# A decoder trunk on one core: the gated norm's sums of squares with ones as the stationary operand, four groups on four quarters of a bank, and one set of roots per layer

## The chip, the cores and the metric

The kernel runs on one core of a Trainium2 chip. The metric is the device time of one execution in microseconds (us); less is better. TensorE (PE; its weight loads are listed apart as PEld), VectorE (DVE), ScalarE (ACT), GpSimd (POOL) and the DMA queues each work through their own instructions in order, and wait for each other through semaphores.

## The reference, cut to what matters

Two layers of a hybrid trunk over 256 tokens of 1024 channels. Each layer normalises the stream, projects it with one wide matrix, runs three token mixers side by side (a Mamba-2 scan, sliding-window attention, forgetting attention), projects each mixer's output to 1024 channels, merges them with sigmoid gates and adds an output projection to the stream. The change lies at the end of the Mamba branch, in its gated norm over four groups of 256 channels:

```python
def grouped_rms_norm(y, w, groups):
    b, s, d = y.shape
    yf = y.astype(jnp.float32).reshape(b, s, groups, d // groups)
    yf = yf * lax.rsqrt(jnp.mean(yf * yf, axis=-1, keepdims=True) + NORM_EPS)
    return (yf.reshape(b, s, d) * w.astype(jnp.float32)).astype(y.dtype)
...
    y = y.reshape(b, s, SSM_INNER) * jax.nn.silu(z)
    return grouped_rms_norm(y, norm_w, SSM_GROUPS)
...
        branch = jnp.einsum('bsiw,iwd->bsid', ys, w_proj[layer])
```

So each token needs one root for each of the four groups, eight numbers a partition when the 256 tokens lie as two tiles of 128.

## The kernel before, in words

**Weights.** Weight matrices come from HBM in pieces of 1024 numbers a partition (`raw`). Each piece is split into a rounded part on ScalarE (`hi`, line 268) and the rest on VectorE (`lo`, line 269), and each dense product is made of three passes over such parts. Six buffers each hold raw, hi and lo; four pieces at most are split ahead, and a piece is released when its last matmul is written down.

**Order.** TensorE's order is the program's. The dense units are written one behind the other. Smaller work (attention, the scan, the norms) is a generator: `launch` puts it on a list with a due time on a clock that `mm` and `transpose` (lines 90 to 101) add up, and `pump`, called within and behind dense units, lets due generators write their next step. `drain(br)` runs all that is left of one kind. The other engines' orders are set by a scheduler from priorities.

**The gated norm.** The eight units `u_z` of the Mamba branch (two blocks of 128 channels to a group) each multiply the scan's output, channels on partitions and 256 tokens along the row, by the gate and square it on ScalarE (line 850). Behind every second unit VectorE adds two squares into one (line 853), and `group_norm` is launched with a delay of 6.5 us. For one group it does, on TensorE, two fp32 matmuls of two columns (the squares of 128 tokens stationary, two columns of ones moving), so that the sums come out with tokens on partitions; then a scale on VectorE (line 866), a power of -0.5 on GpSimd (869), and three small steps on VectorE (871, 872, 874) that refine the root into the tile `gr`. Four groups in two layers make eight such sets.

**The projection.** Two gate units (512 columns, 128 tokens each; line 942 adds the bias, 943 is the tanh) stand between the last `u_z` and `u_proj_groups`, which first drains what is left of the norms. For each of two token tiles it makes the four groups' products, six dense matmuls of 512 columns each, alternately in the pools `mm` (three PSUM banks) and `mx` (five). ScalarE evicts the first group with its root as the scale (line 985), VectorE adds the other three with theirs (987). Then `merge` adds the branch to the others (1001 and 1002).

In the profile's names `ones` is the tile of ones, `L` any work tile, `mm` and `mx` PSUM banks, `pp` attention probabilities. An fp32 matmul leaves two records in the trace, a dense one (rounded parts) or a transpose leaves one.

Of the kernel before, what the change touches and what calls it, by code (L numbers as in the profile page):

```python
# [13 lines left out]
AF = mybir.ActivationFunctionType  # L14
ALU = mybir.AluOpType

P = 128
# [7 lines left out]
D_SOFT, D_SOFT2, D_EVAC, D_SSD, D_SSD2 = 7.0, 3.0, 3.0, 8.0, 3.0  # L25
D_K, D_Q, D_QK, D_G0, D_FOX, D_BDMA, D_BIAS = 6.0, 5.5, 2.0, 8.0, 0.0, 4.0, 2.0
D_SEL, D_CONST, D_NWB = 2.5, 1.5, 10.0
D_GN1, D_CUM, D_H, D_M = 6.5, 12.0, (4.8, 7.0), 5.0
BUDGET = 1.35
T_PP, T_SSD, T_BIAS = 1, 1, 1  # L30
N_RAW, N_SPLIT = 6, 6
# [13 lines left out]
def hybrid_trunk(  # L45
# [29 lines left out]
    def pmx():  # L75
        return PS("mx", 5)
# [14 lines left out]
    def mm(o, a, b, **kw):  # L91
        n = b.free_size()
        if a.dtype == F32R:
            clock["t"] += max(0.094, n / 2350.0)
        else:
            clock["t"] += max(0.2, n / 587.0) * (0.5 if a.free_size() == 64 else 1.0)
        nc.tensor.matmul(o, a, b, **kw)  # L97

    def transpose(o, a, i):
# [731 lines left out]
    def u_z(y, br, u, c):  # L831
        def f(w):
            p = chan(y, w, c)
            if u == 0 and br != 0:
                y.sz[br] = T("L8", [P, NK, S])
            if u == 0 and br == 0:
                y.yh[br] = T("L8", [P, 2, NK, P], F32R)
                y.yl[br] = T("L8", [P, 2, NK, P], F32R)
            th = T("L1", [P, S])
            act(halves(th), p, AF.Tanh, scale=0.5)  # L840
            y.zdone.add((br, u))
            if br != 0:
                stt(halves(y.sz[br][:, u, :]), halves(th), 1.0, p, op0=ALU.add, op1=ALU.mult)
            else:
                drain(0)
                sz = T("L1", [P, S])
                stt(halves(sz), halves(th), 1.0, p, op0=ALU.add, op1=ALU.mult)
                tt(y.xs[:, u, :], y.xs[:, u, :], sz, op=ALU.mult)
                sq = T("L1", [P, S])
                act(sq, y.xs[:, u, :], AF.Square)  # L850
                y.sq.append(sq)
                if u % 2 == 1:
                    tt(y.sq[-2], y.sq[-2], y.sq[-1], op=ALU.add)
                    launch(3 if u < 4 else 4, group_norm(y, u // 2, y.sq[-2]), D_GN1)
                yh, yl, src = y.yh[0][:, :, u, :], y.yl[0][:, :, u, :], halves(y.xs[:, u, :])
                act(yh, src, AF.Copy, scale=y.vec[:, 80 + u:81 + u])
                stt(yl, src, y.vec[:, 80 + u:81 + u], yh.bitcast(F32), op0=ALU.mult, op1=ALU.subtract)
            pump()
        return f

    def group_norm(y, g, q0):
        p = pmx()
        for t in range(2):
            mm(p[:, 2 * t:2 * t + 2], q0[:, t * P:(t + 1) * P], ones[:, 0:2], start=True, stop=True)
        v = T("sm", [P, 8])
        ts(v[:, 0:4], p[:, 0:4], 1.0 / 256, 4 * EPS, op0=ALU.mult, op1=ALU.add)  # L866

        r0 = T("sm", [P, 8])
        nc.gpsimd.tensor_tensor(r0[:, 0:4], v[:, 0:4], mhalf[:, 0:4], op=ALU.pow)  # L869
        a = T("sm", [P, 8])  # L870
        tt(a[:, 0:4], r0[:, 0:4], v[:, 0:4], op=ALU.mult)
        tt(a[:, 0:4], a[:, 0:4], r0[:, 0:4], op=ALU.mult)
        r = T("gr", [P, 4], bufs=4)
        stt(r, a[:, 0:4], -3.0, r0[:, 0:4], op0=ALU.add, op1=ALU.mult)
        y.gr[g] = r
        yield 0.0


# [89 lines left out]
    def u_proj_groups(y, c, t):  # L968

        def f(w):  # L970
            drain(3)
            drain(4)
            q = T("L2", [P, 512])
            for g in range(4):
                p = pmm() if g % 2 == 0 else pmx()
                n = 0
                for k in (2 * g, 2 * g + 1):
                    for a, b in ((y.yh[0], w.hi), (y.yl[0], w.hi), (y.yh[0], w.lo)):
                        mm(p, still(a, t, k), in_turn(b(k)), start=(n == 0), stop=(n == 5))
                        n += 1  # L980
                if w.last:
                    release(w, g + 1)
                r = y.gr[g][:, 2 * t:2 * t + 1]
                if g == 0:
                    act(halves(q), ordered(p), AF.Copy, scale=r)
                else:
                    stt(halves(q), ordered(p), r, halves(q), op0=ALU.mult, op1=ALU.add)
                if g == 1:
                    pump()
            merge(y, 0, c, t, halves(q))  # L990
            pump()
        return f
# [122 lines left out]
    for y in layers:  # L1115
        l = y.l
        w = w_in[l]
        y.gate, y.qT, y.ckT, y.sz, y.yh, y.yl, y.sq, y.h, y.ss, y.var, y.zdone, y.cqdone, y.gr = {}, {}, {}, {}, {}, {}, [], {}, {}, {}, set(), {}, {}

        def cols(c0, n=256):  # L1120
            return sub([(0, w[:, c0:c0 + n])], n)

        def z1(c0, br, b):
            op(cols(c0 + 256 * b), u_z(y, br, 2 * b, 0), u_z(y, br, 2 * b + 1, P))

        def zs(c0, br):
            for b in range(4):
                z1(c0, br, b)

        def gates_proj(br):  # L1130
            def g(b):
                c = 512 * b
                op(cols(C_G + D * br + c, 512), u_gate(y, br, c, 0), u_gate(y, br, c, 1))

            def p(b):
                c = 512 * b
                if b == 0 and br != 0:
                    op(None, lambda y=y: split_late(y, br))
                i = sub([(0, w_proj[l, br, :, c:c + 512])], 512)
                if br == 0:  # L1140
                    op(i, u_proj_groups(y, c, 0), u_proj_groups(y, c, 1))
                else:
                    op(i, u_proj(y, br, c, 0), u_proj(y, br, c, 1))
            seq = [(g, 0), (p, 0), (g, 1), (p, 1)]
            if br == 0:
                seq = [(lambda b: z1(C_ZA, 0, b), b) for b in range(4)] + seq
            return [lambda f=f, b=b: f(b) for f, b in seq]

        if l == 0:
            k, v = cols(C_BK), cols(C_BV)  # L1150
            op(k, u_bkv(y, 0, 0, [lambda j=j: second_rows(j) for j in range(2)]))
            op(k, u_bkv(y, 0, 1))
            op(v, u_bkv(y, 256, 0), u_bkv(y, 256, 1))
            op(None, lambda: layer_consts(y0))
            for c in (0, 2):
                op(cols(C_BQ + 256 * c, 512), u_bq(y, c, 0), u_bq(y, c, 1))
        else:
            kv, q0 = cols(C_BK, 512), cols(C_BQ)
            op(None, lambda: drain(5))
            op(kv, u_bkv(y, 0, 0))  # L1160
            op(q0, u_bq(y, 0, 0))
            op(None, lambda: drain(6))
            op(kv, u_bkv(y, 0, 1))
            op(q0, u_bq(y, 0, 1))
            for c, n in ((1, 512), (3, 256)):
                op(cols(C_BQ + 256 * c, n), u_bq(y, c, 0), u_bq(y, c, 1))
        op(None, lambda y=y: layer_vec(y))
        op(sub([(0, w[:, C_DT:C_DT + 16]), (16, w[:, C_CF:C_CF + 16])], 32), u_small(y))
        zs(C_ZB, 1)
        heavy = [(C_B + 256 * b, 8 + 2 * b) for b in range(4)] + [(C_XS + 256 * b, 2 * b) for b in range(4)]  # L1170
        gp = gates_proj(1)
        lights = [lambda: None, lambda: op(cols(C_CV, 512), u_cv(y, 0, 0), u_cv(y, 0, 1))]
        lights += [lambda: None, lambda: op(cols(C_CV + 512, 512), u_cv(y, 512, 0), u_cv(y, 512, 1))]
        lights += [gp.pop(0), lambda: None, gp.pop(0), lambda: None]
        for (c0, u), light in zip(heavy, lights):
            op(cols(c0), u_conv(y, u, 0), u_conv(y, u + 1, P))
            light()
        for f in gp:
            f()

        for b, zb in enumerate(((), (0,), (1,), (2, 3))):
            op(cols(C_CK + 256 * b), u_ck(y, 2 * b, 0), u_ck(y, 2 * b + 1, P))
            op(cols(C_CQ + 256 * b), u_cq(y, 2 * b, 0), u_cq(y, 2 * b + 1, P))
            if b == 1:
                op(None, load_final if l + 1 == L else lambda: layer_consts(layers[1]))
            for z in zb:
                z1(C_ZC, 2, z)
        for f in gates_proj(0):
            f()
        for f in gates_proj(2):  # L1190
            f()
        o = [sub([(0, w_out[l, :, c:c + n])], n) for c, n in ((0, 256), (256, 512), (768, 256))]
        pieces_out[l] = o[0]
        op(o[0], u_out2(y, 0))
        for t in range(2):
            for i, c in ((1, 256), (2, 768)):
                op(o[i], u_out(y, c, t, i))
# [91 lines left out]
```

## Time and profile before

| | us |
|---|---|
| median of 3 runs (834.16 to 834.62) | 834.62 |
| the profiled execution | 834.18 |
| its span | 832.3 |
| TensorE busy | 820.6 |
| VectorE busy | 656.4 |
| ScalarE busy | 504.6 |
| GpSimd busy | 127.2 |

The span is the time from the first to the last instruction; 1.9 us of the profiled execution lie around it. A row of the profile's timeline has the start, the length from the first start to the last end of like instructions in a row, the engine, the line, and the operation with what it writes and reads, partitions by elements (for a matmul rows*columns of the array that are in use, then what is moved), the count, and, where the engine sat idle before, for how long and what ended it. Layer 1 repeats layer 0's stage about 407 us later.

### The profile page before, as it was taken

What the parts mean: (1) busy time and instruction counts of PE and PEld (TensorE: products, weight loads), DVE (VectorE), ACT (ScalarE), POOL (GpSimd) and SP (SyncE); (2) the same over time, 40 slices, a digit from 0 to 9 for tenths busy, and PEclk for the clock granted to TensorE, in tenths of its full rate; (3) what the DMA queues carried; (4) which work ended last, traced back from release to release, by engine and by line L of the source; (5) the groups of instructions that cost most, each with busy time, mean ns of one, the idle gap of its engine ahead of it and who ended that gap; (6) DMA issues with size and microseconds to landing.
All of it is one profiled execution on the core that took longest, in us unless ns stands there. A gap on an engine that the chain in (4) does not pass through costs nothing.

```text
span 832.3 us, 15656 instructions
## 1 busy us (share of the span) xinstructions
PE 820.6 (99%) x5800; PEld 748.7 (90%) x5800; DVE 656.4 (79%) x1355; ACT 504.6 (61%) x970; POOL 127.2 (15%) x167
## 2 busy tenths in 40 slices
PE   7999999999999999999999999999999999999996
PEld 7999888989999998888989998898899999988896
DVE  5788997998776788875788889889968668888665
ACT  6566777665666675543555667775457666655442
POOL 7411300000130211100014121000003110121000
PEclk9999999999999999999999999999999999999999
DMA  9946564567474756676687575456756565667632
GB/s 301 273 147 184 179 202 165 176 217 227 131 208 136 240 167 189 216 216 201 209 245 216 146 212 174 152 182 196 244 165 185 167 181 150 189 216 215 215 104 74
DMA packets 123739, 158.39 MB, mean 190 GB/s; under 512 B 12800, under 2 KB 84208, under 8 KB 123664
## 3 DMA queue, kind: packets, MB, share of 16 engines
q1 hardware_dynamic: 109456, 140.79, 55.3%
q10 hardware_dynamic: 14160, 16.49, 6.7%
q8 instruction: 45, 0.74, 0.4%
q14 instruction: 30, 0.25, 0.1%
q0 software_dynamic: 48, 0.13, 0.0%
HBM read 155.22 MB, written 2.16 MB: 189 GB/s over the span
## 4 chain that ended last, share of the span: by engine, by line
PE 97%; DMA 1%; ACT 0%; DVE 0%; POOL 0%; SPq 0%; issue 0%; POOLq 0%
PE mm L97 83%; PE mx L97 11%; PE mx L101 4%; DMA raw<-in_w_in_dram 1%; POOL lo L1221 0%; ACT hi L1220 0%; ACT L L1079 0%; DVE L L269 0%; ACT L L268 0%; POOLq L1285 0%; ACT L L219 0%; DVE L L1062 0%; SPq L163 0%; DVE L L1067 0%; SPq L164 0%
## 5 line engine op out<-in xcount | busy, mean ns | idle before, releaser
L269 DVE TENSOR_TENSOR lo<-raw,hi 128x1024 fp32r<-128x1024 f32 x252 | 310.1, 1243 | 71.0 <-ACT hi L268 65.3
L97 PE MATMUL mm<-hi,L 128*128 128x512 f32 (+1 forms) x1280 | 354.3, 363 | 1.9 <-ACT hi L1220 1.4
L268 ACT ACTIVATE hi<-raw 128x1024 fp32r<-128x1024 f32 x252 | 264.0, 1055 | 91.6 <-PE mm L97 77.5
L97 PE MATMUL mm<-L,hi 128*128 128x256 f32 x1792 | 316.9, 278 | 0.0
L97 PEld LDWEIGHTS mm<-L,hi 128*128 128x128 f32 x1792 | 277.5, 192 | 5.9 <-issue 3.4
L97 PEld LDWEIGHTS mm<-hi,L 128*128 128x128 f32 x1280 | 229.5, 190 | 30.9 <-issue 2.0
L97 PE MATMUL mm<-L,lo 128*128 128x256 f32 x896 | 246.4, 275 | 0.0
L97 PE MATMUL mm<-lo,L 128*128 128x512 f32 (+1 forms) x640 | 229.5, 360 | 0.2 <-POOL lo L1221 0.2
L97 PEld LDWEIGHTS mm<-L,lo 128*128 128x128 f32 x896 | 171.9, 192 | 0.2
L97 PEld LDWEIGHTS mm<-lo,L 128*128 128x128 f32 x640 | 121.3, 190 | 14.2 <-POOL lo L1221 0.5
L919 POOL TENSOR_SCALAR_AFFINE_SELECT bias<-bias 128x128 f32<-128x128 f32 x64 | 39.0, 642 | 268.9 <-DMA bias<-cumd 182.4
L779 DVE SCALAR_TENSOR_TENSOR L<-L,vec,L 128x255 f32<-128x255 f32 (+2 forms) x96 | 46.9, 489 | 6.4 <-ACT L L776 5.0
L97 PE MATMUL mx<-L,L 128*64 128x128 f32 (+1 forms) x384 | 36.5, 332 | 0.0
L97 PEld LDWEIGHTS mx<-L,L 128*64 128x64 f32 x384 | 23.8, 136 | 11.9 <-issue 2.7
L651 ACT ACTIVATE pp<-pp,nm 128x128 f32<-128x128 f32 x64 | 25.1, 393 | 13.6 <-DVE nm L644 13.5
L576 ACT ACTIVATE pp<-pp,nm 128x128 f32<-128x128 f32 x64 | 28.2, 443 | 8.3 <-DVE nm L570 8.3
L943 ACT ACTIVATE L<-L 128x512 f32<-128x512 f32 x24 | 15.0, 627 | 28.4 <-DVE L L942 28.1
L840 ACT ACTIVATE L<-mm 128x256 f32<-128x256 f32 x48 | 18.0, 376 | 20.6 <-PE mm L97 20.3
L782 ACT ACTIVATE L<-L 128x256 f32<-128x256 f32 x32 | 13.3, 417 | 26.6 <-DVE L L779 26.2
L676 POOL TENSOR_SCALAR_AFFINE_SELECT L<-L 128x256 f32<-128x256 f32 x16 | 10.3, 641 | 112.4 <-ACT L L674 112.4
L644 DVE CUSTOM_DVE_ANT_0 pp<-mx,wmask,nsink 128x128 f32<-128x128 f32 x64 | 24.1, 412 | 1.8 <-PE mx L97 1.8
L869 POOL TENSOR_TENSOR sm<-sm,mhalf 128x4 f32<-128x4 f32 x8 | 12.0, 1496 | 76.8 <-DVE sm L866 76.8
(181 smaller groups left out, 820.4 us busy)
## 6 DMA issues: line engine op xcount, KB each, us to landing
raw<-in_w_in_dram SPq DMA_DIRECT2D x200, 512.0 KB, 4.7
raw<-in_w_proj_dram SPq DMA_DIRECT2D x48, 512.0 KB, 4.5
raw<-in_w_out_dram SPq DMA_DIRECT2D x16, 512.0 KB, 5.0
L<-cumd ACTq DMA_DIRECT2D x8, 512.0 KB, 4.0
bias<-cumd ACTq DMA_DIRECT2D x16, 256.0 KB, 3.7
L<-in_gate_bias_dram ACTq DMA_DIRECT2D x12, 256.0 KB, 3.7
L<-in_x_dram SPq DMA_DIRECT2D x2, 512.0 KB, 4.8
nwb<-in_norm_w_dram SPq DMA_DIRECT2D x1, 512.0 KB, 5.3
```

What stands on the lines that cost most here:

```text
L97: nc.tensor.matmul(o, a, b, **kw)
L101: nc.tensor.transpose(o, a, i)
L268: keep(act)(hi, src, AF.Copy)
L269: keep(tt)(lo, src, hi.bitcast(F32), op=ALU.subtract)
L576: act(pp[:, i, sl], pp[:, i, sl], AF.Exp, scale=-1.0, bias=nm[:, e:e + 1], accum_out=sums[:, e:e + 1])
L644: nc.vector.tensor_tensor_reduce(out=pp[:, i, sl], in0=score(p, i, b), in1=m, scale=-0.125, scalar=ns[:, i:i + 1], op0=ALU.add, op1=ALU.mi ...
L651: act(pp[:, i, sl], pp[:, i, sl], AF.Exp, scale=-1.0, bias=nm[:, e:e + 1], accum_out=sums[:, e:e + 1])
L779: stt(a[:, s:S], x_[:, 0:S - s], y.vec[:, 16 * j + u:16 * j + u + 1], a[:, s:S], op0=ALU.mult, op1=ALU.add)
L782: act(th, a, AF.Tanh)
L840: act(halves(th), p, AF.Tanh, scale=0.5)
L919: nc.gpsimd.affine_select(out=bias[:, i, dst], in_=bias[:, i, src], compare_op=ALU.is_ge, fill=NEG, base=0, pattern=[[-1, P]], channel_mul ...
L943: act(g, g, AF.Tanh, scale=0.5)
```

## The change

`group_norms` takes the place of `group_norm`: it is launched once a layer, behind the last `u_z`. It keeps the four sums of squares until then. Four matmuls with 32 columns of ones as the stationary operand and 256 columns of a group's sums as the moving one write to the partitions 0 to 31, 32 to 63, 64 to 95 and 96 to 127 of one bank. ScalarE copies them, and at the next step two transposes bring the tokens to the partitions. One scale, one power and three small steps over 128x8 then make all eight roots, in place of four sets over 128x4. The clock that sets due times counts a matmul with 32 columns at a quarter, and the kind numbered 4 goes.

```diff
-D_GN1, D_CUM, D_H, D_M = 6.5, 12.0, (4.8, 7.0), 5.0
+D_GN1, D_GN2, D_CUM, D_H, D_M = 6.5, 2.5, 12.0, (4.8, 7.0), 5.0
...
-            clock["t"] += max(0.2, n / 587.0) * (0.5 if a.free_size() == 64 else 1.0)
+            clock["t"] += max(0.2, n / 587.0) * {64: 0.5, 32: 0.25}.get(a.free_size(), 1.0)
...
-                    launch(3 if u < 4 else 4, group_norm(y, u // 2, y.sq[-2]), D_GN1)
+                    if u == NK - 1:
+                        launch(3, group_norms(y), D_GN1)
...
-    def group_norm(y, g, q0):
+    def group_norms(y):
+        p = pmx()
+        for g in range(4):
+            mm(p[32 * g:32 * g + 32, 0:S], ones[:, 0:32], y.sq[2 * g], start=True, stop=True)
+        sums = T("L1", [P, S])
+        act(sums, p[:, 0:S], AF.Copy)
+        yield D_GN2
         p = pmx()
         for t in range(2):
-            mm(p[:, 2 * t:2 * t + 2], q0[:, t * P:(t + 1) * P], ones[:, 0:2], start=True, stop=True)
+            transpose(p[:, t * P:(t + 1) * P], sums[:, t * P:(t + 1) * P], ident)
         v = T("sm", [P, 8])
-        ts(v[:, 0:4], p[:, 0:4], 1.0 / 256, 4 * EPS, op0=ALU.mult, op1=ALU.add)
-
+        ts(v, p[:, 0:2 * P].rearrange("p (e r) -> p e r", r=32)[:, :, 0], 1.0 / 256, 4 * EPS,
+           op0=ALU.mult, op1=ALU.add)
         r0 = T("sm", [P, 8])
-        nc.gpsimd.tensor_tensor(r0[:, 0:4], v[:, 0:4], mhalf[:, 0:4], op=ALU.pow)
+        nc.gpsimd.tensor_tensor(r0, v, mhalf, op=ALU.pow)
         a = T("sm", [P, 8])
-        tt(a[:, 0:4], r0[:, 0:4], v[:, 0:4], op=ALU.mult)
-        tt(a[:, 0:4], a[:, 0:4], r0[:, 0:4], op=ALU.mult)
-        r = T("gr", [P, 4], bufs=4)
-        stt(r, a[:, 0:4], -3.0, r0[:, 0:4], op0=ALU.add, op1=ALU.mult)
-        y.gr[g] = r
+        tt(a, r0, v, op=ALU.mult)
+        tt(a, a, r0, op=ALU.mult)
+        y.gr = T("rs", [P, 8], bufs=4)
+        stt(y.gr, a, -3.0, r0, op0=ALU.add, op1=ALU.mult)
         yield 0.0
...
             drain(3)
-            drain(4)
...
-                r = y.gr[g][:, 2 * t:2 * t + 1]
+                r = y.gr[:, 4 * t + g:4 * t + g + 1]
```

**TensorE.** Before, in layer 0, the second of the four groups: an attention output (`mx_4101`, on 64 columns), the two matmuls of the norm, and the next dense unit.

```order
L97 MATMUL mm_4054<-L_25_153,hi_3889 128x256
L97 MATMUL mx_4101<-L_727_3945,L_273_1357 64x256 x2
L97 MATMUL mx_4101<-L_743_4033,L_273_1357 64x128 x2
L97 MATMUL mx_4101<-L_743_4033,L_273_1357 64x256
L97 MATMUL mx_4101<-L_745_4040,L_273_1357 64x256
L97 MATMUL mx_4101<-L_745_4040,L_273_1357 64x128 x2
L97 MATMUL mx_4111<-ones_86,L_725_3936 128x2 x2
L97 MATMUL mm_4123<-L_24_152,hi_3963 128x256
```

Now the norm's matmuls stand together in the middle of the second gate unit, three quarters through the two (`mm_4210`):

```order
L97 MATMUL mm_4210<-hi_4073,L_25_153 128x512
L97 MATMUL mm_4210<-lo_4074,L_24_152 128x512
L97 MATMUL mx_4235<-L_710_3844,ones_86 32x256
L97 MATMUL mx_4235<-L_725_3936,ones_86 32x256
L97 MATMUL mx_4235<-L_742_4027,ones_86 32x256
L97 MATMUL mx_4235<-L_759_4119,ones_86 32x256
L97 MATMUL mm_4210<-hi_4146,L_24_152 128x512
```

Twelve dense matmuls later come the transposes, ahead of the projection's first group (`mm_4282`):

```order
L97 MATMUL mm_4210<-hi_4164,L_24_152 128x512
L97 MATMUL mm_4210<-hi_4164,L_25_153 128x512
L97 MATMUL mm_4210<-lo_4165,L_24_152 128x512
L101 MATMUL mx_4269<-ident_71,L_782_4240 128x128 x2
L97 MATMUL mm_4282<-hi_4217,L_706_3837 128x512
L97 MATMUL mm_4282<-hi_4217,L_707_3838 128x512
```

The eight groups of two-column matmuls are gone; besides, the attention output `mx_4101` stands 24 dense matmuls later than it did. Nothing else of TensorE's order moves, and layer 1 is changed in the same way.

**ScalarE**, from the first gate's tanh (line 943 before, 949 now) to the projection's first eviction (985, now 990). Before:

```order
L268 ACTIVATE hi_4289<-raw_4071 128x1024
L943 ACTIVATE L_788_4243<-L_788_4243 128x512
L268 ACTIVATE hi_4301<-raw_4089 128x1024
L268 ACTIVATE hi_4353<-raw_4174 128x1024
L268 ACTIVATE hi_4367<-raw_4192 128x1024
L985 ACTIVATE L_808_4310<-mm_4311,gr_4052 128x512
```

Now, with the copy of the sums at line 867:

```order
L949 ACTIVATE L_773_4207<-L_773_4207 128x512
L268 ACTIVATE hi_4248<-raw_4059 128x1024
L268 ACTIVATE hi_4260<-raw_4077 128x1024
L867 ACTIVATE L_782_4240<-mx_4235 128x256
L1036 DMA L_922_4898<-in_x_dram 128x256
L1036 DMA L_925_4902<-in_x_dram 128x256
L268 ACTIVATE hi_4324<-raw_4150 128x1024
L268 ACTIVATE hi_4338<-raw_4168 128x1024
L1036 DMA L_951_5034<-in_x_dram 128x256
L1036 DMA L_972_5137<-in_x_dram 128x256
L949 ACTIVATE L_789_4266<-L_789_4266 128x512
L990 ACTIVATE L_795_4281<-mm_4282,rs_4279 128x512
```

The copy stands behind the second of four splits, the second gate's tanh has come ahead of the first eviction, and four loads of the stream (line 1031 before, then ahead of these rows) stand among them.

**VectorE**, from the splits of the projection's weights to its first scaled sum (line 987, now 992). Before, with the last group's scale and refinement (866, 871, 872, 874) among the splits:

```order
L269 TENSOR_TENSOR lo_4290<-raw_4071,hi_4289 128x1024
L866 TENSOR_SCALAR sm_4274<-mx_4271 128x4
L269 TENSOR_TENSOR lo_4302<-raw_4089,hi_4301 128x1024
L871 TENSOR_TENSOR sm_4278<-sm_4276,sm_4274 128x4
L269 TENSOR_TENSOR lo_4354<-raw_4174,hi_4353 128x1024
L872 TENSOR_TENSOR sm_4278<-sm_4278,sm_4276 128x4
L942 TENSOR_TENSOR L_807_4307<-mm_4246,L_786_4216 128x512
L874 SCALAR_TENSOR_TENSOR gr_4281<-sm_4278,sm_4276 128x4
L269 TENSOR_TENSOR lo_4368<-raw_4192,hi_4367 128x1024
L987 SCALAR_TENSOR_TENSOR L_808_4310<-mx_4319,gr_4121,L_808_4310 128x512
```

Now:

```order
L269 TENSOR_TENSOR lo_4249<-raw_4059,hi_4248 128x1024
L269 TENSOR_TENSOR lo_4261<-raw_4077,hi_4260 128x1024
L269 TENSOR_TENSOR lo_4325<-raw_4150,hi_4324 128x1024
L948 TENSOR_TENSOR L_789_4266<-mm_4210,L_771_4180 128x512
L873 TENSOR_SCALAR sm_4272<-mx_4269 128x8
L269 TENSOR_TENSOR lo_4339<-raw_4168,hi_4338 128x1024
L878 TENSOR_TENSOR sm_4276<-sm_4274,sm_4272 128x8
L879 TENSOR_TENSOR sm_4276<-sm_4276,sm_4274 128x8
L881 SCALAR_TENSOR_TENSOR rs_4279<-sm_4276,sm_4274 128x8
L992 SCALAR_TENSOR_TENSOR L_795_4281<-mx_4290,rs_4279,L_795_4281 128x512
```

The splits and the gate's sum keep their order; the scale comes behind the gate's sum with one split between it and the refinement, and the refinement's three steps stand together right ahead of the first scaled sum. The rows of the three earlier groups, further up, are gone.

More of the change, by code (lines that the diff above doesn't have):

```diff
@@ L1117, in hybrid_trunk @@
         w = w_in[l]
-        y.gate, y.qT, y.ckT, y.sz, y.yh, y.yl, y.sq, y.h, y.ss, y.var, y.zdone, y.cqdone, y.gr = {}, {}, {}, {}, {}, {}, [], {}, {}, {}, set(), {}, {}
+        y.gate, y.qT, y.ckT, y.sz, y.yh, y.yl, y.sq, y.h, y.ss, y.var, y.zdone, y.cqdone = {}, {}, {}, {}, {}, {}, [], {}, {}, {}, set(), {}
         def cols(c0, n=256):
```

## The prediction

> **What bounds the kernel now.** I read the busy shares first, then the chain that ended last, then TensorE's waits. The first two are on the page:
>
> ```profile
> span 832.3 us, 15656 instructions
> PE 820.6 (99%) x5800; PEld 748.7 (90%) x5800; DVE 656.4 (79%) x1355; ACT 504.6 (61%) x970; POOL 127.2 (15%) x167
> PEclk9999999999999999999999999999999999999999
> PE 97%; DMA 1%; ACT 0%; DVE 0%; POOL 0%; SPq 0%; issue 0%; POOLq 0%
> ```
>
> TensorE is busy for 99% of the span at the full clock, and 97% of the chain is TensorE's. The third view is TensorE's waits from 14 us to the end; these two lines are the whole answer:
>
> ```profile
> PE mm L97 <- ACT L L268: 0.2, 1, 0.2
> PE mm L97 <- DVE L L269: 0.2, 1, 0.2
> ```
>
> So after the start TensorE waits twice, 0.4 us in all (both at the turn of the layers). While that stays so, the span moves by what TensorE's own stream gains or loses. What the change does to VectorE, ScalarE and GpSimd counts only if it makes TensorE wait.
>
> **Term 1, what goes: eight groups of matmuls with two columns.** A busy time counts overlapping records twice, so I take prices from start times. This is the third group of layer 0, between two dense stretches:
>
> ```profile
> 311.07 0.28 PE L97 MATMUL mm<-L,hi 128*128 128x256 f32 x1
> 311.18 0.51 PE L97 MATMUL mx<-ones,L 128*128 128x2 f32 x4
> 311.55 0.68 PE L97 MATMUL mm<-hi,L 128*128 128x512 f32 x2
> 312.06 0.38 PE L97 MATMUL mm<-lo,L 128*128 128x512 f32 x1
> ```
>
> The group (two fp32 matmuls, two records each) starts at 311.18, and the third dense matmul behind it at 312.06, 0.88 us later. Two dense matmuls of 512 columns belong to that time. Their pitch is read from the stretch in the next fence: 102.29 to 102.94 is three of them, 0.217 each. So a group costs 0.88 - 0.43 = 0.45 us, though it streams two columns: with so few, the load of 128 weight columns is what takes the time. The first group, behind transposes, comes out the same:
>
> ```profile
> 300.60 0.51 PE L97 MATMUL mx<-ones,L 128*128 128x2 f32 x4
> 300.97 0.36 PE L97 MATMUL mm<-L,hi 128*128 128x256 f32 x1
> 301.16 0.28 PE L97 MATMUL mm<-L,lo 128*128 128x256 f32 x1
> ```
>
> From 300.60 to 301.16 is 0.56, less one dense matmul of 256 columns (0.11, as from 311.07 to 311.18): 0.45. Four groups a layer make **1.8 us**.
>
> **Term 2, what comes: four matmuls on quarters of the array.** The stationary operand is 32 columns of ones, the moving one 256 columns of sums. No row of before has four quarters at work. The nearest are the attention outputs, on halves (128*64), here between dense matmuls of 512:
>
> ```profile
> 100.00 0.38 PE L97 MATMUL mm<-lo,L 128*128 128x512 f32 x1
> 100.31 1.52 PE L97 MATMUL mx<-L,L 128*64 128x256 f32 x16
> 101.76 0.70 PE L97 MATMUL mm<-hi,L 128*128 128x512 f32 x2
> 102.29 0.38 PE L97 MATMUL mm<-lo,L 128*128 128x512 f32 x1
> 102.51 0.59 PE L97 MATMUL mm<-hi,L 128*128 128x512 f32 x2
> 102.94 0.38 PE L97 MATMUL mm<-lo,L 128*128 128x512 f32 x1
> ```
>
> From 100.00 to 102.29 is 2.29, less three dense matmuls (0.65): 1.64 us for eight fp32 matmuls of two records each, four of 256 columns and four of 128. What one record streams is read from transposes: six records of 128 columns from 299.95 to 300.60, 0.109 each.
>
> ```profile
> 299.95 0.82 PE L101 MATMUL mx<-ident,pp 128*128 128x128 f32 x6
> ```
>
> A record of 256 fp32 columns is then 0.218. One behind the other, the 16 records would take 8 x 0.218 + 8 x 0.109 = 2.6 us; two side by side take 1.31. The measured 1.64 is the second, plus 0.33 for going into the form with fewer columns and back. A close window shows how they stand beside each other:
>
> ```profile
> 303.82 0.44 PE L97 MATMUL mx<-L,L 128*64 128x256 f32 x2
> 303.82 0.65 PE L97 MATMUL mx<-L,L 128*64 128x256 f32 x4
> ```
>
> Two records that take 0.43 alone are both over 0.44 us after the first began, and four (both records of two matmuls) after 0.65. So the halves run side by side from the first record on.
>
> For four quarters there are then four prices, each with the 0.33: all four together, 2 x 0.218 + 0.33 = 0.77 us; two at a time, 4 x 0.218 + 0.33 = 1.20; a staircase in which each matmul's first record runs beside the second of the one before, 5 x 0.218 + 0.33 = 1.42; one after the other, 8 x 0.218 + 0.33 = 2.07. I take **0.77**, since nothing in the rows on halves sets a limit at two. The lower end, with the switch at nothing, is 0.44.
>
> Here a rule of the Trainium skill speaks against the change. The page "TensorE: Matmul & The Clock Gate", Part 3, says that matmuls start and end strictly in program order; for fp32 matmuls of two records that would make the staircase. The rows on halves disagree (two records within 0.01 us of each other at the start, where the second record of the same matmul can't be), unless the two records of a matmul are not neighbours in that order. The same part gives a measured speedup of 3.07 for four tiles; as an estimate by that figure the four would stream in 1.74 / 3.07 = 0.57 us instead of 0.44, and the saving would be 0.26 us smaller in all.
>
> **Term 3: two transposes a layer**, of the form above: 2 x 0.109 = **0.22 us**.
>
> **Sum.** A layer loses 1.8 and gains 0.77 + 0.22 = 0.99: 0.80 us less, **1.6 us for the two**. The rest of TensorE's order stays, but for one attention output that moves behind 24 dense matmuls; it stands between dense matmuls before and after. The profiled execution took 834.18 us, so 832.58. The runs lie at 834.16 and 834.62, the median at the upper; 1.6 off the median is 833.02. I predict **833.0**.
>
> **What hides the rest.** *The copy of the sums* on ScalarE (0.37 us, as the copies of 128x256 at L840) must end before the transposes, or TensorE waits. Between quarters and transposes stand twelve dense matmuls, 2.6 us. ScalarE's rows there before:
>
> ```profile
> 318.09 1.06 ACT L268 ACTIVATE hi<-raw 128x1024 fp32r<-128x1024 f32 x1 [1.74 <-PE mm L97]
> 319.06 0.61 ACT L943 ACTIVATE L<-L 128x512 f32<-128x512 f32 x1
> 319.58 1.04 ACT L268 ACTIVATE hi<-raw 128x1024 fp32r<-128x1024 f32 x1
> 321.17 1.07 ACT L268 ACTIVATE hi<-raw 128x1024 fp32r<-128x1024 f32 x1 [0.56 <-ACT hi L268]
> 322.47 1.06 ACT L268 ACTIVATE hi<-raw 128x1024 fp32r<-128x1024 f32 x1 [0.23 <-PE mm L97]
> 323.93 0.69 ACT L985 ACTIVATE L<-mm,gr 128x512 f32<-128x512 f32 x1 [0.41 <-PE mm L97]
> ```
>
> In the new order the copy stands behind the second split of this stretch. TensorE frees that split's buffer when the quarters begin; it takes 1.05, the copy 0.37, so the sums lie ready 1.5 to 1.8 us after the quarters began, against 0.77 + 2.6 = 3.4. **Cover: 1.6 us.** Without it, what is lacking would be TensorE's wait, once a layer.
>
> *The roots.* Before, three groups had theirs long ahead, and the last came as late as it could:
>
> ```profile
> 321.35 1.85 POOL L869 TENSOR_TENSOR sm<-sm,mhalf 128x4 f32<-128x4 f32 x1 [8.25 <-DVE sm L866]
> 323.24 0.16 DVE L871 TENSOR_TENSOR sm<-sm,sm 128x4 f32<-128x4 f32 x1 [0.90 <-POOL sm L869]
> 324.56 0.68 DVE L942 TENSOR_TENSOR L<-mm,L 128x512 f32<-128x512 f32 x1
> 325.23 1.22 DVE L269 TENSOR_TENSOR lo<-raw,hi 128x1024 fp32r<-128x1024 f32 x1
> 326.37 0.74 DVE L987 SCALAR_TENSOR_TENSOR L<-mx,gr,L 128x512 f32<-128x512 f32 x1
> ```
>
> Now all four need the transposes, and the first eviction (L985, ScalarE) waits for them. Counted from the transposes' start: up to 0.5 until they can be read, VectorE finishing a split and the gate's sum (1.22 + 0.68), the scale (0.15), the power on GpSimd (the rows of 128x4 run from 1.0 to 1.94; 128x8 is not in the trace, and I take 1.9), three small steps (0.5): about 4.9. ScalarE evicts by 5.6. TensorE needs that bank again only when the two others of the pool of three are filled, at the seventh group of six dense matmuls (every second group goes to the other pool): after 0.22 + 6 x 1.3 = 8.0 us. **Cover: 2.4 us.** Behind the waiting eviction ScalarE's queue holds the next split, and that one waited for TensorE anyway:
>
> ```profile
> 328.94 1.06 ACT L268 ACTIVATE hi<-raw 128x1024 fp32r<-128x1024 f32 x1 [3.04 <-PE mm L97]
> ```
>
> Three us idle there, so the split isn't late. VectorE's first scaled sum starts about 1 us later relative to TensorE; it had idle time of 0.5 us behind these sums, and its sixteen small steps and three waits on GpSimd become four steps and one wait.
>
> **The rivals.**
>
> *Fewer than four at once* (two at a time, or the staircase): 0.43 to 0.65 us dearer a layer, a saving of 0.3 to 0.7 us, **833.9 to 834.3**. For it: nothing in the trace has more than two. Against it: the halves show no trace of waiting for each other.
>
> *One after the other, the other side*: if quarters overlapped as little as matmuls on the full array do, a layer would pay 2.07 + 0.22 for the 1.8 it loses, 0.5 us more, and the time would be **835.6**, slower. It decides from 1.58 us for the four upward (1.8 - 0.22). Against it speak the halves.
>
> *Roots too late*: beyond the cover of 2.4 us each us costs one a layer. Two more splits of VectorE ahead of the small steps (2.4) and a power of twice the length (1.9) would bring 1.9 us of wait a layer, 3.8 - 1.6 = 2.2 us more than before, **836.8**. The new order has one split there, so this needs a stage that runs quite unlike before.
>
> *It doesn't do what it says*: the transposes wait for the sums. Beyond 1.6 us of cover; at 0.8 us of wait a layer the gain is gone, **834.6**.
>
> **How the numbers follow.** All four together 0.75; fewer at once 0.12; one after the other 0.05; roots too late 0.05; sums too late 0.03. The range runs from the lower end (0.44 for the four: 1.1 us a layer, 832.3, and 0.3 of the 0.46 us between the levels of the runs) to the staircase: **832.0 to 834.3**, which leaves out 0.13. A difference of 0.2%, 1.67 us, is about what a measurement of this kernel can tell from no change. My forecast of 1.6 lies just short of it, and the runs of before are 0.46 apart, so the likeliest case falls on both sides: **faster 0.40** (half of that case and little else), **same 0.53** (the other half, fewer at once, one after the other, sums late), **slower 0.07**.
>
> **What would show it.** The quarters' rows: eight records on 128*32 that start within 0.3 us if all four run together, and the third dense matmul behind them 0.77 + 0.43 us after the first of them. Transposes with no wait on ScalarE's copy. TensorE's waits still at 0.4 us. The eviction at L990 later relative to the projection's start by 2 to 4 us, with TensorE streaming through it. I am wrong if the quarters take over 1 us, or if TensorE waits for `mx<-ident,L` or on a bank in the first projection of the Mamba branch.

## The result and the profile after

The kernel after takes **832.86 us** (median of 16 runs, 832.35 to 834.32), the kernel before 834.26 in the same comparison (16 runs, 834.10 to 835.83). The ratio is **0.9981**, 95% interval 0.9974 to 0.9988: some 1.4 to 1.6 us, 1.6 having been forecast. The profiled execution took 832.96 us, 1.22 less than that of before; its span is 1.1 shorter (831.2 for 832.3).

The page of the kernel after, its span, the busy times and the chain that ended last:

```profile
span 831.2 us, 15603 instructions
PE 819.1 (99%) x5788; PEld 745.2 (90%) x5788; DVE 654.2 (79%) x1331; ACT 504.2 (61%) x972; POOL 121.1 (15%) x161
PE 96%; DMA 2%; DVE 1%; issue 0%; ACT 0%; POOL 0%; SPq 0%; POOLq 0%; DVEq 0%
```

TensorE is the bound as before. VectorE has 24 instructions and 2.2 us less to do, GpSimd six instructions and 6.1 us less; neither figure says anything of the time, since TensorE did not wait for either there.

TensorE's timeline around the new stage in layer 0 (start, length, engine, line, operation):

```profile
318.00 0.38 PE L97 MATMUL mm<-lo,L 128*128 128x512 f32 x1
318.31 0.64 PE L97 MATMUL mx<-L,ones 128*32 128x256 f32 x8
...
319.42 0.38 PE L97 MATMUL mm<-lo,L 128*128 128x512 f32 x1
...
321.36 0.38 PE L97 MATMUL mm<-lo,L 128*128 128x512 f32 x1
321.58 0.39 PE L101 MATMUL mx<-ident,L 128*128 128x128 f32 x2
...
322.24 0.38 PE L97 MATMUL mm<-lo,L 128*128 128x512 f32 x1
```

The price is read as in the prediction, by starts. From 318.00 to 319.42 is 1.42; three dense matmuls (0.65) belong to it, the first row's and two that are left out, so the four quarters cost **0.77**. From 321.36 to 322.24 is 0.88, less the same 0.65: the transposes cost **0.23**. The layer pays 1.00 for the 1.79 that it lost (four groups at 0.447). Layer 1 comes out the same within 0.01.

A window of 0.04 us, from 318.30 to 318.34, shows how many records have begun by then:

```profile
318.31 0.42 PE L97 MATMUL mx<-L,ones 128*32 128x256 f32 x4
```

Four, each some 7 ns behind the other in the trace's records; the other four (the second records of the same matmuls) begin together 0.24 us later. So four run at once, first all the first records and then all the second.

The saving is then 1.6 us for the two layers, and the span of the profiled execution shows 1.1. The rest went in two places. One is the start: the attention outputs that began at 100.31 before begin later, ahead of anything that was changed.

```profile
100.47 1.52 PE L97 MATMUL mx<-L,L 128*64 128x256 f32 x16
```

That is 0.16 us, and differs from execution to execution: in the second profile of the kernel after (e9_after) they begin at 100.30. TensorE's wait for GpSimd's split (line 1226, 0.8 us, until 16.00), the one new line in its waits from 14 us on, is part of the start too.

The other is **a new wait at the turn of the layers**, which the prediction did not have. With the later start, TensorE is 0.6 us ahead of before from the stage on, and a load of the residual stream is issued 0.6 us sooner, but it does not land 0.6 us sooner. ScalarE's queue in the kernel after issues it here (DMA issues are listed as ACTq):

```profile
410.56 0.45 ACTq L1036 DMA_DIRECT2D L<-in_x_dram  x1
```

VectorE's sum with it (line 1067) waits for the load, 5.7 us after the issue, and holds what stands behind it:

```profile
416.23 0.69 DVE L1067 TENSOR_TENSOR L<-mm,L 128x512 f32<-128x512 f32 x1 [0.53 <-DMA L<-in_x_dram]
...
417.97 0.68 DVE L269 TENSOR_TENSOR L<-mx,L 128x512 fp32r<-128x512 f32 x1
```

Behind it on VectorE stands its half of the next layer's token split (line 269), which ends at 418.65. TensorE needs that, and its weight load (listed apart as PEld) begins late, at 418.70 (the row names line 223, which ends only at 418.71); the matmuls show what it costs:

```profile
418.70 0.19 PEld L97 LDWEIGHTS mm<-hi,L 128*128 128x128 f32 x1 [0.36 <-DVE sm L223]
418.26 0.93 PE L97 MATMUL mm<-hi,L 128*128 128x512 f32 x2
419.03 0.38 PE L97 MATMUL mm<-lo,L 128*128 128x512 f32 x1
```

From 418.26 to 419.03 two matmuls take 0.77 us (0.76 unrounded), where 0.43 is their time: **0.33 us lost**. Of that, 0.23 lies ahead of the matmul that waited and 0.10 behind it: the next start follows it by 0.32 us and not by 0.217, as behind the waits of e5_late and e6_late_early below. Before, the load was issued at 411.19 and VectorE's sum began at 416.30 with no wait for it:

```profile
416.30 0.68 DVE L1062 TENSOR_TENSOR L<-mm,L 128x512 f32<-128x512 f32 x1
```

Together 1.60 - 0.16 - 0.33 = 1.11 us, against 1.12 by the spans. The other 0.10 of the 1.22 lies outside the span.

### The profile page after: what moved, and what is told of

The parts are those of the page before. It is cut to its first block, busy times and chain, and to the rows that moved or that the text cites. A ratio compares the mean times of both kernels' runs of the same rounds, so it can differ in the third digit from the quotient of the medians.

```text
span 831.2 us, 15603 instructions
## 1 busy us (share of the span) xinstructions
PE 819.1 (99%) x5788; PEld 745.2 (90%) x5788; DVE 654.2 (79%) x1331; ACT 504.2 (61%) x972; POOL 121.1 (15%) x161
## 4 chain that ended last, share of the span: by engine, by line
PE 96%; DMA 2%; DVE 1%; issue 0%; ACT 0%; POOL 0%; SPq 0%; POOLq 0%; DVEq 0%
PE mm L97 81%; PE mx L97 11%; PE mx L101 4%; DMA raw<-in_w_in_dram 1%; DMA L<-in_x_dram 1%; POOL lo L1226 0%; DVE L L269 0%; DVE lo L269 0%; ACT hi L1225 0%; DVE L L1067 0%; ACT L L219 0%; ACT L L1084 0%; ACT L L268 0%; POOLq L1290 0%; SPq L163 0%
## 5 line engine op out<-in xcount | busy, mean ns | idle before, releaser
L101 PE MATMUL mx<-ident,L 128*128 128x128 f32 x148 | 22.5, 275 | 0.3 <-DVE L L1237 0.3
```

Source lines behind the costliest of these rows:

```text
L101: nc.tensor.transpose(o, a, i)
```

## The experiments

**Theory A**: the gain is the difference of TensorE's own stream and nothing else; four quarters run at once and cost 2 x 0.218 + 0.33 us. **Theory B**, the rival: the gain comes from VectorE and GpSimd, which have one set of roots a layer to make in place of four. The edits are shown against the kernel after. Prices of stages are read by starts, as above: from the dense matmul ahead of the stage to the third start behind it, less three dense matmuls (0.65), of which two are left out of the rows. A wait is priced in the same way, up to the third start behind it. Layer 1 agrees within 0.01 us, unless it is said otherwise.

### e1_halves: the four sums on halves of the array

```diff
-            mm(p[32 * g:32 * g + 32, 0:S], ones[:, 0:32], y.sq[2 * g], start=True, stop=True)
-        sums = T("L1", [P, S])
-        act(sums, p[:, 0:S], AF.Copy)
+            mm(p[64 * (g % 2):64 * (g % 2) + 64, S * (g // 2):S * (g // 2) + S], ones[:, 0:64], y.sq[2 * g],
+               start=True, stop=True)
+        sums = T("L2", [P, 2 * S])
+        act(sums, p, AF.Copy)
...
-            transpose(p[:, t * P:(t + 1) * P], sums[:, t * P:(t + 1) * P], ident)
+            for j in range(2):
+                transpose(p[:, (2 * t + j) * P:(2 * t + j + 1) * P], sums[:, j * S + t * P:j * S + (t + 1) * P], ident)
...
```

> The four matmuls on halves of the array (64 columns of ones), two groups beside each other and two behind them, four transposes. Theory A (the gain is TensorE's stream alone, and the quarters run four at a time): the matmuls cost 4 x 0.218 + 0.33 = 1.20 us a layer in place of 0.77, the transposes 0.44 in place of 0.22, so 0.65 us more a layer and 1.3 us more than the change: 834.2, the gain over before (834.3) nearly gone. Theory B (the gain comes from the one set of roots: fewer small steps on VectorE and fewer waits on GpSimd): as the change, 832.9.

Measured: 833.92 us, ratio 0.9997 (0.9988 to 1.0006). TensorE's timeline of this kernel:

```profile
317.86 0.38 PE L97 MATMUL mm<-lo,L 128*128 128x512 f32 x1
318.16 1.08 PE L97 MATMUL mx<-L,ones 128*64 128x256 f32 x8
...
319.71 0.38 PE L97 MATMUL mm<-lo,L 128*128 128x512 f32 x1
```

From 317.86 to 319.71 is 1.85, less 0.65: 1.20, as "two at a time" gives, and 0.43 more than on quarters. The roots are batched here as in the kernel after, and nearly all of the gain is gone. That is theory A. The time lies 0.3 under the expected one, which was counted from the 832.9 of the kernel after, and so held that kernel's wait at the turn of the layers; this profile does not have it.

### e2_full: 128 columns of ones, one matmul after another

All four groups take the roots of the first here: the roots of the other three are left out.

```diff
-        p = pmx()
+        p, p2 = pmx(), pmx()
...
-            mm(p[32 * g:32 * g + 32, 0:S], ones[:, 0:32], y.sq[2 * g], start=True, stop=True)
+            mm((p, p2)[g // 2][:, g % 2 * S:g % 2 * S + S], ones, y.sq[2 * g], start=True, stop=True)
```

> The four matmuls on the full array (128 columns of ones), one behind the other, into two banks; the copy and the transposes as in the change, so that all four groups take the roots of the first (left out: the roots of the other three). Theory A: 4 x 2 x 0.218 = 1.74 us a layer with no change of form, in place of 0.77, 0.97 us more a layer: 834.8, slower than before by 0.5 us. Theory B: as the change, 832.9.

Measured: 834.40 us, ratio 1.0002 (0.9994 to 1.0011). TensorE's timeline:

```profile
317.84 0.38 PE L97 MATMUL mm<-lo,L 128*128 128x512 f32 x1
318.06 1.89 PE L97 MATMUL mx<-L,ones 128*128 128x256 f32 x8
...
320.21 0.38 PE L97 MATMUL mm<-lo,L 128*128 128x512 f32 x1
```

2.37 less 0.65 is 1.72 us: eight records in a row at 0.215, with no change of form. The time lies 0.4 under the expected one; the price is as expected. This stage costs 0.95 us more than the quarters, 1.9 us for the two layers; the measured difference to the kernel after is 1.5, and here too the wait at the turn of the layers (0.33 in the profile of the kernel after) is not in the profile.

### e3_roots: one set of roots, the sums as before

```diff
-            mm(p[32 * g:32 * g + 32, 0:S], ones[:, 0:32], y.sq[2 * g], start=True, stop=True)
-        sums = T("L1", [P, S])
-        act(sums, p[:, 0:S], AF.Copy)
-        yield D_GN2
-        p = pmx()
-        for t in range(2):
-            transpose(p[:, t * P:(t + 1) * P], sums[:, t * P:(t + 1) * P], ident)
+            for t in range(2):
+                e = 2 * (4 * t + g)
+                mm(p[:, e:e + 2], y.sq[2 * g][:, t * P:(t + 1) * P], ones[:, 0:2], start=True, stop=True)
...
```

> One set of roots a layer as in the change, but the sums made as before (squares stationary, two columns moving, eight fp32 matmuls in a row). Theory A: 16 weight loads of 0.112 us are 1.79 us a layer, the same as before: 834.3, no gain. Theory B: all of the gain, 832.7 to 832.9.

Measured: 834.35 us, ratio 1.0001 (0.9992 to 1.001). TensorE's timeline:

```profile
317.67 0.38 PE L97 MATMUL mm<-lo,L 128*128 128x512 f32 x1
317.88 1.84 PE L97 MATMUL mx<-ones,L 128*128 128x2 f32 x16
...
320.10 0.38 PE L97 MATMUL mm<-lo,L 128*128 128x512 f32 x1
```

2.43 less 0.65 is 1.78 us, what the four groups cost one by one. Batched roots alone bring nothing that can be measured, and **theory B falls**.

### e4_twice: the quarters twice

```diff
-        for g in range(4):
+        for g in (0, 1, 2, 3, 0, 1, 2, 3):
```

> The change with its four quarter matmuls made twice over. Theory A, with 0.33 us for going into the form and back paid once: the second four add 2 x 0.218 = 0.44 us a layer, 0.9 in all: 833.7; on TensorE 1.20 us from the dense stream's point of view in place of 0.77. If the quarters did not run four at a time the second four would add 0.87 (two at a time) or more, 834.6 and up. Theory B: as the change, 832.9.

Measured: 833.40 us, ratio 0.9993 (0.9984 to 1.0002). TensorE's timeline (the profiled execution took 835.05; TensorE was 1.6 us later than in the kernel after from 18 us on, ahead of the stage):

```profile
319.55 0.38 PE L97 MATMUL mm<-lo,L 128*128 128x512 f32 x1
319.86 1.07 PE L97 MATMUL mx<-L,ones 128*32 128x256 f32 x16
...
321.40 0.38 PE L97 MATMUL mm<-lo,L 128*128 128x512 f32 x1
```

1.85 less 0.65 is 1.20: the second four add 0.43, which is two records of 0.218 and not eight. The remaining 0.33 us of the 0.77 (1.20 less four records of 0.218) is paid once, for the change of form.

### e5_late: the power on GpSimd twice

```diff
         nc.gpsimd.tensor_tensor(r0, v, mhalf, op=ALU.pow)
+        nc.gpsimd.tensor_tensor(r0, v, mhalf, op=ALU.pow)
```

> The change with GpSimd's power made twice over into the same tile, so that the roots come 2.6 us later. By the changed kernel's trace the first eviction ends at 328.5 and TensorE needs its bank at 329.5, 1.0 us of cover. Theory A with that cover: TensorE waits 1.6 us a layer on the bank, up to 2.0 if VectorE's splits then come late as well: 836.1 to 836.9. If GpSimd's lateness is hidden further on (the bank is not what ends the wait): 832.9.

Measured: 834.18 us, ratio 0.9997 (0.9988 to 1.0007), a miss in size. GpSimd's timeline gives the reason, the second power is cheaper than the first:

```profile
324.47 2.58 POOL L876 TENSOR_TENSOR sm<-sm,mhalf 128x8 f32<-128x8 f32 x1 [37.17 <-DVE sm L873]
327.13 1.65 POOL L877 TENSOR_TENSOR sm<-sm,mhalf 128x8 f32<-128x8 f32 x1
```

So ScalarE's first eviction (line 991 here) comes 1.67 us later than in the kernel after, 329.49 for 327.82, and TensorE waits for it at the bank of the seventh group:

```profile
329.29 0.38 PE L97 MATMUL mx<-lo,L 128*128 128x512 f32 x1
330.23 0.70 PE L97 MATMUL mm<-hi,L 128*128 128x512 f32 x2 [0.56 <-ACT L L991]
330.76 0.38 PE L97 MATMUL mm<-lo,L 128*128 128x512 f32 x1
```

The start at 330.23 is 0.94 behind the one before it, 0.72 over the pitch (0.68 in layer 1). Of 1.67 us, 0.72 reach TensorE, so **about 1.0 us was cover** in the kernel after. By the third start behind it, at 330.76, TensorE has lost 0.82 (0.79). The wait stands where the prediction put it; the cover is less than half of what it said.

### e6_late_early: the same, and the norm launched 3 us earlier

```diff
-D_GN1, D_GN2, D_CUM, D_H, D_M = 6.5, 2.5, 12.0, (4.8, 7.0), 5.0
+D_GN1, D_GN2, D_CUM, D_H, D_M = 3.5, 2.5, 12.0, (4.8, 7.0), 5.0
...
+        nc.gpsimd.tensor_tensor(r0, v, mhalf, op=ALU.pow)
```

> As the run before (power made twice), but the sums are launched with a due time of 3.5 us in place of 6.5, so that quarters and transposes stand twelve dense matmuls (2.6 us) earlier. If lateness of the roots against the bank is what costs, TensorE's wait on the bank is gone. In its place the quarters, which now stand at the end of the first gate unit, wait for the last sum of squares (VectorE makes it at 316.2 in the changed kernel's trace, TensorE is there at 315.6): 0.7 us a layer, 834.3. If the extra work on GpSimd costs by itself: as the run before.

Measured: 835.28 us, ratio 1.0009 (1.0 to 1.0017), another miss. TensorE's timeline:

```profile
315.52 0.38 PE L97 MATMUL mm<-lo,L 128*128 128x512 f32 x1
315.83 1.21 PE L97 MATMUL mx<-L,ones 128*32 128x256 f32 x8
...
317.50 0.38 PE L97 MATMUL mm<-lo,L 128*128 128x512 f32 x1
...
327.44 0.38 PE L97 MATMUL mx<-lo,L 128*128 128x512 f32 x1
328.41 0.70 PE L97 MATMUL mm<-hi,L 128*128 128x512 f32 x2 [0.59 <-DVE L L949]
328.94 0.38 PE L97 MATMUL mm<-lo,L 128*128 128x512 f32 x1
```

The stage costs 1.33 (1.98 less 0.65): the last squares are not there yet, 0.57 us of wait. The transposes do come 2 us sooner (319.66, left out of the rows, for 321.58). But a wait stays, now for the gate's sum on VectorE: the start at 328.41 is 0.75 over the pitch (0.71 in layer 1), and by 328.94 TensorE has lost 0.85 (0.81). VectorE's timeline shows why:

```profile
326.14 0.17 DVE L879 TENSOR_TENSOR sm<-sm,sm 128x8 f32<-128x8 f32 x1 [3.30 <-POOL sm L877]
...
327.67 0.68 DVE L949 TENSOR_TENSOR L<-mm,L 128x512 f32<-128x512 f32 x1
```

The refinement steps now stand ahead of the gate's sum in VectorE's order, and VectorE stands still for 3.30 us at the first of them. An earlier launch moves the wait to another bank and does not take it away.

### e7_onehot: the full array, rounded sums, one matmul a group

The sums of squares are written rounded (F32R), so a matmul leaves one record. The stationary operand is 128 columns, ones in the group's 32 and zeros elsewhere, and the four matmuls accumulate into one bank.

```diff
...
-                sq = T("L1", [P, S])
+                sq = T("L1", [P, S], F32R) if u % 2 == 0 else T("L1", [P, S])
...
-            mm(p[32 * g:32 * g + 32, 0:S], ones[:, 0:32], y.sq[2 * g], start=True, stop=True)
+            mm(p[:, 0:S], fin["sel"][:, 96 - 32 * g:224 - 32 * g], y.sq[2 * g], start=(g == 0), stop=(g == 3))
```

> The sums of squares rounded for one-record matmuls, and four matmuls on the full array with a stationary operand of 128 columns whose 32 columns of the group are one and the others zero, added up in one bank; copy, transposes and roots as in the change. Theory A: 4 x 0.112 = 0.45 us a layer with no change of form, in place of 0.77: 0.32 us less a layer, 832.2. If the form of the quarters cost nothing beyond its records (0.44), no difference: 832.9.

Measured: 832.47 us, ratio 0.9976 (0.9967 to 0.9984). TensorE's timeline:

```profile
317.70 0.38 PE L97 MATMUL mm<-lo,L 128*128 128x512 f32 x1
317.91 0.65 PE L97 MATMUL mx<-L,sel 128*128 128x256 f32 x4
...
318.83 0.38 PE L97 MATMUL mm<-lo,L 128*128 128x512 f32 x1
...
320.77 0.38 PE L97 MATMUL mm<-lo,L 128*128 128x512 f32 x1
321.24 0.44 PE L101 MATMUL mx<-ident,L 128*128 128x128 f32 x2
...
321.94 0.38 PE L97 MATMUL mm<-lo,L 128*128 128x512 f32 x1
```

The sums cost 0.48 us (1.13 less 0.65), near the expected 0.45. But the transposes start 0.47 behind the dense matmul ahead of them, 0.25 over the pitch, because the copy of the sums is not done, and cost 0.52 with it (320.77 to 321.94, less 0.65). The layer pays 1.00, as on quarters. ScalarE's timeline shows that the copy (line 873 here) did not come sooner, though the sums did:

```profile
320.82 0.36 ACT L873 ACTIVATE L<-mx 128x256 f32<-128x256 f32 x1
```

It stands behind a tanh and two splits (left out of the rows). A stage that is 0.29 us shorter meets the same copy, and the cover is gone.

### e8_short and e9_after: no copy and no transposes, beside the kernel after

The old form of the sums with rounded operands, so that 8 records of two columns a layer do what 16 did, all in one place and with one set of roots; and, on the same chip, the kernel after without an edit.

```diff
...
-                sq = T("L1", [P, S])
+                sq = T("L1", [P, S], F32R) if u % 2 == 0 else T("L1", [P, S])
...
-            mm(p[32 * g:32 * g + 32, 0:S], ones[:, 0:32], y.sq[2 * g], start=True, stop=True)
-        sums = T("L1", [P, S])
-        act(sums, p[:, 0:S], AF.Copy)
-        yield D_GN2
-        p = pmx()
-        for t in range(2):
-            transpose(p[:, t * P:(t + 1) * P], sums[:, t * P:(t + 1) * P], ident)
+            for t in range(2):
+                e = 2 * (4 * t + g)
+                mm(p[:, e:e + 2], y.sq[2 * g][:, t * P:(t + 1) * P], fin["two"], start=True, stop=True)
...
```

> The old form of the sums (the squares' sums as the stationary operand, two columns of ones moving), all eight of a layer in one place, with the sums of squares and the ones rounded to the one-record form (F32R): 8 records of two columns a layer in place of 16, no copy of sums and no transposes; one set of roots as in the kernel after. Theory A (a two-column record costs the loading of 128 weight columns, and the gain is the sum of TensorE's stream alone): half of the 1.79 us that the 16 records of two columns took, 0.89 us a layer, 0.90 less than before, 832.5 us; as the refinement can begin about 3 us sooner, TensorE waits for no root. Rival (a rounded record of two columns is not shorter than a dense one of 512 columns, 0.217): 1.74 us a layer, 834.2 us.

> The kernel after, unchanged, beside the variant with rounded sums on the same chip: 0.99 us a layer, 0.2 us more than the variant in all by theory A (832.7 to 833.0 us); 1.5 us less than it by the rival.

Measured: **832.33 us** for the variant, ratio 0.9978 (0.9969 to 0.9987); 832.83 for the kernel after, ratio 0.9981 (0.9973 to 0.999). The variant's TensorE timeline:

```profile
317.79 0.38 PE L97 MATMUL mm<-lo,L 128*128 128x512 f32 x1
318.00 0.95 PE L97 MATMUL mx<-two,L 128*128 128x2 f32 x8
...
319.33 0.38 PE L97 MATMUL mm<-lo,L 128*128 128x512 f32 x1
```

1.54 less 0.65 is 0.89 us, exactly half of e3_roots. Eight records cost 0.11 each, as sixteen did: the price is per record, each with its own load of 128 weight columns. Whether the load alone sets it is not shown, since records and loads were halved together. The two kernels differ by 0.50 us where the stage gives 0.2. The rest fits the wait at the turn of the layers: in this second profile of the kernel after it is there again, and in the variant's it isn't. The kernel after, VectorE's timeline:

```profile
416.21 0.69 DVE L1067 TENSOR_TENSOR L<-mm,L 128x512 f32<-128x512 f32 x1 [0.68 <-DMA L<-in_x_dram]
```

TensorE loses 0.48 us behind it (the second matmul behind the one at 418.10 starts at 419.01, 0.91 later, where 0.43 is the time of two). The variant, which reaches the place still sooner:

```profile
415.48 0.69 DVE L1066 TENSOR_TENSOR L<-mm,L 128x512 f32<-128x512 f32 x1
```

It does not wait for the load there. Issued at 410.24, its load had landed within 5.24 us; in the kernel after it took 5.67 and 5.81. Of the eleven profiles, the two of the kernel after alone show this wait; in the others the sum begins 5.05 to 5.24 us after the issue, in e7_onehot too, which issues the load at 410.27. Whether the change makes this load slower or the two profiles drew slow ones isn't settled, and taking the wait away wasn't tried on the chip.

### The sums side by side

A layer before pays 1.79 us for the sums. The worked time is the median of before in the same comparison (834.27 for e1 to e4, 834.41 for e5 to e7, 834.18 for e8 and e9), plus twice the difference:

| kernel | sums | transposes | wait behind | worked | measured |
|---|---|---|---|---|---|
| e1_halves | 1.21 | 0.44 | | 833.99 | 833.92 |
| e2_full | 1.73 | 0.22 | | 834.59 | 834.40 |
| e3_roots | 1.79 | | | 834.27 | 834.35 |
| e4_twice | 1.20 | 0.22 | | 833.53 | 833.40 |
| e5_late | 0.77 | 0.22 | 0.81 | 834.43 | 834.18 |
| e6_late_early | 1.33 | 0.22 | 0.84 | 835.61 | 835.28 |
| e7_onehot | 0.48 | 0.52 | | 832.83 | 832.47 |
| e8_short | 0.89 | | | 832.38 | 832.33 |
| e9_after | 0.77 | 0.23 | | 832.60 | 832.83 |

Five agree within 0.2 us. e9_after came 0.23 higher, where the wait at the turn of the layers (0.48 in its profile) is not in the sum. e5_late, e6_late_early and e7_onehot came 0.25, 0.33 and 0.36 lower. These three were measured beside the same runs of before, whose median (834.41) lies 0.14 to 0.23 above the other two, so part of what they share lies in that base; the rest stays open.

## Why the prediction was right, and where it was not

**What goes** (0.45 a group): 0.447 a group, four of them 1.79 a layer. The cause given, the weight load, fits but is not shown by itself: e8_short halves records and loads together, and half of them cost half.

**What comes** (0.77, chosen among 0.77, 1.20, 1.42 and 2.07): 0.77. The sign was put a little off: the third dense matmul starts 1.11 us behind the first quarter and not 1.20, since 0.09 of the change of form lies ahead of that quarter. The halves had already shown matmuls side by side from the first record on, and nothing limited it to two. The staircase needs strict order of the two records of each matmul; four first records within 0.02 us refute it. The Trainium skill's rule on program order ("TensorE: Matmul & The Clock Gate", Part 3) therefore doesn't bind the two records of one fp32 matmul here to stand next to each other. Its speedup of 3.07 stands there for four row tiles, and these are four column tiles: the estimate by it was 0.57 us of streaming, and e4_twice measured 0.43 for four more.

**Transposes** (0.22): 0.22 and 0.23.

**The cover of the sums' copy: mis-sized.** The step said that the copy would end 1.6 us ahead of the transposes. ScalarE in the kernel after:

```profile
318.68 0.63 ACT L949 ACTIVATE L<-L 128x512 f32<-128x512 f32 x1 [2.48 <-DVE L L948]
319.21 1.04 ACT L268 ACTIVATE hi<-raw 128x1024 fp32r<-128x1024 f32 x1
...
321.11 0.37 ACT L867 ACTIVATE L<-mx 128x256 f32<-128x256 f32 x1
```

The copy ends at 321.48, and the weight load of the transposes already waits for it:

```profile
321.53 0.20 PEld L101 LDWEIGHTS mx<-ident,L 128*128 128x128 f32 x2 [0.19 <-ACT L L867]
```

The transposes still start on the pitch, at 321.58, and cost 0.23 for 0.22. So **nothing was left of the cover**: a sign that the prediction had named, TensorE waiting for `mx<-ident,L`, is there in the weight load, and it was by luck that it cost no more than 0.01 us. The step counted the second split from the moment TensorE frees its buffer. But ScalarE stood still for 2.48 us ahead of the first gate's tanh, which waits for VectorE's sum, and the splits and the copy stand behind the tanh. The order of the rows was known; what the tanh waits for was not followed. e7_onehot confirms it: 0.29 us less of TensorE work ahead, 0.3 us more for the transposes.

**The cover of the roots: mis-sized**, 2.4 us foretold and about 1.0 measured (e5_late). GpSimd's power of 128x8 was taken at 1.9 us:

```profile
324.54 2.58 POOL L876 TENSOR_TENSOR sm<-sm,mhalf 128x8 f32<-128x8 f32 x1 [37.31 <-DVE sm L873]
```

It took 2.58, and VectorE's scale came at 324.30, 2.7 us behind the transposes. The first eviction (line 990) begins at 327.82, 6.2 us behind their start where 5.6 was to be its end; relative to the projection's start it came 4.6 us later than before (327.82 after 321.73, for 323.93 after 322.44), not 2 to 4. The group that takes the bank begins at 329.58, 1.1 us behind the eviction's end. The cover held, so neither slip cost any time; the rival "roots too late" was 1.0 us away and not 2.4.

**The rest of the stream stays**: not quite. The load at the turn of the layers took back 0.33 and 0.48 us in the two profiles of the kernel after. With that and a start of 0.16 us more, the 1.6 of the sum became 1.1 in the span of the profiled execution; by the medians it is 1.4. That the forecast of 833.0 was right within 0.2 us is partly luck: it was set from the upper median of the few runs shown, 0.36 above the median of 16, and the saving was put 0.20 too large; the two errors work against each other.

## What to carry to other kernels

Where one engine is busy for 99% of the span, price an edit by the starts of that engine's rows: a stage's length less the dense matmuls in it gave every variant here within 0.4 us. A record that streams two columns cost 0.11 us here, as much as one that streams 128, so count records first: rounding the operand halves them and, where that rounding is allowed, needs neither quarters, copy nor transposes (832.33 us for 832.83). Cover is read by following what every instruction ahead in that engine's order waits for, not by adding durations from the moment its buffer is free; and a stage that gets shorter uses up the cover of whatever does not move with it, a copy or a load.

## What was not expected of the hardware

- Four fp32 matmuls on quarters of the columns run as four first records, 7 ns apart, and then four second ones 0.24 us later. A further four cost 0.43 us, fully four at a time. Going into the form and back costs 0.33 us, once, on quarters as on halves.
- GpSimd's power of 128x8 took 2.58 us behind a long pause and 1.65 us right behind another one (e5_late); of 128x4, 1.0 to 1.94 before.
- The same 256 KB load took at most 5.05 to 5.24 us in nine profiles, and 5.67 and 5.81 us in the two of the kernel after, from issue to the sum that needs it.
